# Block sums in the last up tiles, two 8 KB weight slots, and raw token tiles on GpSimd in a decoder layer

## The chip, the cores and the metric

The kernel runs on one core of one Trainium2 chip. Its time is the device time of one execution in microseconds; lower is better. A core has TensorE (matrix products; PE in the profile, PEld for its weight loads), VectorE (DVE), ScalarE (ACT), GpSimd (POOL) and SyncE (SP), whose queue issues all the large DMAs of this kernel. Each engine runs its own instructions in a fixed order and waits at semaphores for the others.

## The reference, cut to what matters

One layer over 1024 tokens of width 1024, all float32. Three parts add to the residual stream `x`; the change touches the first two.

```python
x = x + 0.5 * (silu(h1 @ w_gate) * (h1 @ w_up)) @ w_down        # FFN1, h1 = rms_norm(x), hidden width 2816
h = rms_norm(x); p = h @ w_in                                   # latents, FoX q, k, v, forget logits, two gates
x = x + (sigmoid(g_mla) * (mla(p) @ w_a) + sigmoid(g_fox) * (fox(p) @ w_b)) @ w_o
x = x + 0.5 * (silu(h2 @ w_gate) * (h2 @ w_up)) @ w_down        # FFN2, h2 = rms_norm(x)
```

Float32 accuracy is kept on 16-bit products by writing each operand as a high and a low half and taking three products: high by high, high by low, low by high.

## The kernel before, in words

**Order on the engines.** The kernel is written as Python that emits instructions. A planner then lays them out per engine: among the instructions whose inputs and buffers are ready in its own model of time, the earliest emitted goes first. So an instruction can be placed well before the point where the code emits it. Three means hold it back: `in_order(engines)` chains everything in a block per engine, `follow(name)` puts one instruction behind a named one on its engine, and buffers: `slot(tag)` takes one of the 8 KB tiles "u" (8 of them), "v", "act" and "wd" (4 each), and an instruction that fills one waits until its last reader is done. PSUM has two double banks "a", three banks "b" and one "g".

**FFN1's start** (`start`, inside `in_order` for ScalarE, VectorE and TensorE). For each of eight token tiles `norm_steps` gives steps: `q` (squares), `s` (scale), `t` (eight transposes into a double bank, L612), `h` (ScalarE copies the bank as 16-bit high half, L620 and L622), `l` (VectorE subtracts to get the low half, L637 and L639) and, for tiles 4 to 7, `r` (`raw`, ScalarE copies the bank once more as float32, L629 and L631). `token_sums` then builds sums of token quarters from high, low and raw tiles on VectorE (L879, L883) for a product scheme that needs seven block products instead of eight.

**FFN1's up part.** The hidden width is cut into 22 tiles of 128. Tiles 2 to 21 go through `tile(j)` in `up_tiles` and `hidden_tile`: seven steps of 12 products each (L1045), with the operands of the next tile made by `pair_sums`: three GpSimd sums (L1020 to L1022), seven splits (L166 on ScalarE, L169 on VectorE), and a GpSimd subtract in between (L1034). GpSimd also multiplies gate and up (L1095) and makes the sums of activations of a pair of tiles (`act_sums`, L841), which SP stores (L845). The last step of a tile runs inside the next one. `extra()` at the end of `tile(j)` carries side work: with k = j - 3 it loads one slice of `w_in` and takes the maximum of the one before (L803), and at chosen k calls `in_scales`, which spreads such maxima over all partitions by small TensorE products (`spread_max`, L200, then L208) and turns them into powers of two with short VectorE instructions. At k = 17 (tile 20) it calls the third and the fourth part one after the other; the fourth first reduces two small vectors (L979).

**FFN1's down part** (`ffn_down`). Two halves of K with five blocks each (CK = 5), seven block products each, so 70 steps of 12 products (L1205). Operands are prepared three steps ahead. A block of `w_down` takes one slot, filled by two DMAs (`down_load`, L929), and three or four GpSimd sums make its combinations t1 to t4 (L1177), emitted at the steps that need them: t1 at i = 0, t2 at i = 1, t3 at i = 3, t4 at i = 5. The first five t1 are held behind products of the last up tiles by `follow`. The old rows of `x` are loaded behind the fifth block (L516).

**Input projection** (`in_proj`, `proj_steps`, TensorE in order). Three groups (queries, keys, values) of eight token tiles, each in two halves `h` of 12 products. `in_weights` loads a group's weights as four DMAs of 512 KB into a ring of two buffers (`stgi`, L1320) and splits each (L166, L169). Between the halves run the chains of FoX queries and keys (`fox_qk`, L1407 to L1420) and of the MLA projections (`mla_proj`, L1549 to L1657).

FFN2 runs the same code as FFN1 on other buffers; its second half of the start is `first_half`.

Of the kernel before, what the change touches and what calls it, by code (L numbers as in the profile page):

```python
# [14 lines left out]
AF = mybir.ActivationFunctionType  # L15
ALU = mybir.AluOpType
AX = mybir.AxisListType
# [47 lines left out]
class Layer:  # L65
    def __init__(self, tc, ins, out):
        self.tc = tc
        self.nc = tc.nc
        self.i = ins
        self.out = out  # L70
        self.bcount = 0
        self.opn = 0
        self.products = []


    def psa(self, name="psa"):
# [348 lines left out]
    def first_half(self, norm, p0):  # L425


        pg, pu = self.psbg(), self.psbg()
        n = {t: self.norm_steps(norm, t) for t in range(4, NT)}
        (wg, wu), (hi, lo) = p0["w"], (norm[k][0] for k in ("hi", "lo"))  # L430
        full = lambda t: [n[t][c]() for c in "hlr"]
        both = lambda t: [n[t][c]() for c in "qs"]
        part = lambda o, w, c: self.part(o, w, hi, lo, c)
        both(4)
        part(pg, wg, "H")
        n[4]["t"]()
# [12 lines left out]
        n[7]["t"]()  # L449
        full(7)  # L450
        part(pu, wu, "L")
        self.mark()
        return pg, pu
# [119 lines left out]
    def norm_steps(self, st, t, engine=None):  # L573
# [50 lines left out]
        def raw():  # L624
            if t >= 4 and st["raw"] is not None:
                for k in (0, 4):
                    o, a = st["raw"].rows(k, 4, s), rows(box["ps"], k)
                    if not late:
                        nc.scalar.copy(o, a)  # L629
                    else:  # L630
                        nc.scalar.activation(o, a, AF.Copy, scale=st["s"])  # L631

        def low():
            for k in (0, 4):
# [137 lines left out]
    def up_tiles(self, norm, name, tags, loads, stats, scales, sumd):  # L772
# [4 lines left out]
        def tile(j, ops, tok, finish, mid):  # L777
            if j + 3 < NH:
                loads[j + 3] = self.pair_load(name, j + 3, tags["w"])
            nxt = iter(())  # L780
            if j + 1 < NH:
                nxt = self.pair_sums(loads.pop(j + 1), stats.pop(j + 1), norm, scales, j + 1)
# [12 lines left out]
            box["even"] = e  # L795
            def extra():
                k = j - 3
                if name == "ffn1":
                    load, n, values = self.injobs
                    if 0 < k <= n + 1:  # L800
                        last = self.latest(mybir.EngineType.DVE)
                        col = 1663 + k if k <= n else 1701
                        self.nc.vector.tensor_reduce(  # L803
                            out=self.spare[:, col:col + 1], in_=box.pop("in"), op=ALU.max, axis=AX.X,
                            apply_absolute_value=True,
                        )
# [21 lines left out]
            )  # L828

        return tile  # L830

    def act_sums(self, a, b, dst, last=False):

# [104 lines left out]
    def in_jobs(self):  # L938
# [14 lines left out]
        def values(slot):  # L953
            st = slot[:, :HEADS * HD].rearrange("p (h d) -> p h d", h=HEADS)
            self.nc.sync.dma_start(st, self.i["mla_w_kvb"][0].rearrange("p (h d) -> p h d", h=HEADS)[:, :, HD:])
            self.nc.sync.dma_start(
                self.spare[:, 1703:1704], self.i["mla_kv_lat_norm"][0].rearrange("(p k) -> p k", k=1)
            )
            return slot[:, :HEADS * HD]

        return load, len(cuts), values
# [1 line left out]
    def in_scales(self, part):  # L963

        v = self.nc.vector
        raw, m, ps = self.spare[:, 1664:1680], self.spare[:, 1680:1692], self.psb("mx")
# [8 lines left out]
        small, all3 = self.spare[:, 1692:1700], self.spare[:, 1700:1703]  # L975
        t, wkv, gkv = (all3[:, k:k + 1] for k in range(3))
        last = self.latest(mybir.EngineType.DVE)
        for o, src in ((t, small), (gkv, self.spare[:, 1703:1704])):
            v.tensor_reduce(out=o, in_=src, op=ALU.max, axis=AX.X, apply_absolute_value=True)  # L979
            self.follow(last)  # L980
        self.spread_max(all3, 3, all3, ps)
        v.tensor_tensor(out=wkv, in0=wkv, in1=gkv, op=ALU.mult)
        s, inv = self.pow2(m, 14, self.ws[:, :36])
# [27 lines left out]
    def pair_sums(self, w, stat, norm, scales, j):  # L1011
# [20 lines left out]
        yield split(a11)  # L1032
        yield split(a12)
        pool(out=a12, in0=a12, in1=s2, op=ALU.subtract)  # L1034
        for src in (a21, s2, a12, s3, a22):
            yield split(src)

# [12 lines left out]
    def hidden_tile(self, ops, tok, e, nxt, finish, then, inv, late, mid, extra, col):  # L1050
# [45 lines left out]
        self.products = (self.products + [nc.cur_bb.bb.instructions[-1].name])[-3:]  # L1096
        prep()
        late()
        extra()
# [11 lines left out]
    def ffn_down(self, x, old, name, tags, tail, pending):  # L1111
# [13 lines left out]
        raw, extra, staged, loaded = {}, {}, {}, {}  # L1125

        def weights(k):
            if k >= KT or k in raw:
                return
            w = self.down_load(name, k, self.slot(tags["raw"][k % len(tags["raw"])]))  # L1130
            loaded[k] = self.latest(mybir.EngineType.SP)
            if k % CK % 2 == 0:
                extra[k] = self.slot(tags["extra"]).rearrange("p (k s n) -> p k s n", k=2, s=2)
            e = extra[k - k % CK % 2][:, k % CK % 2]
            raw[k] = dict(
                b11=w[:, 0, 0], b21=w[:, 1, 0], t1=w[:, 0, 1], b22=w[:, 1, 1], t2=e[:, 0], t3=e[:, 1], t4=w[:, 1, 0],
            )

        def acts(c, i, k):

# [20 lines left out]
        def prep(n):  # L1161
# [10 lines left out]
            a = operand(acts(c, i, k), self.down[c][0], after)  # L1172
            b = operand(w[order[i][1]], self.down[c][1], after)
            made = {0: ("t1", "t1", "b11"), 1: ("t2", "b22", "t1"), 3: ("t3", "t2", "b11"), 5: ("t4", "b21", "t2")}
            if i in made:
                o, u, v = (w[s] for s in made[i])
                nc.gpsimd.tensor_tensor(out=o, in0=u, in1=v, op=ALU.subtract)  # L1177
# [9 lines left out]
        for n, (c, i, k) in enumerate(steps):  # L1187
# [6 lines left out]
                self.down.append(self.down_scale(1, mx))  # L1194
            ready.append(prep(n + ahead))
            if n == 1 and name == "ffn1":
                self.load_x(x, old, range(NT), loaded[CK - 1])
# [99 lines left out]
        v.tensor_tensor(out=d2, in0=d2, in1=tmp, op=ALU.add)  # L1297


    def in_weights(self, name, c0, after=()):  # L1300
# [5 lines left out]
        scale = self.win[("lat", "q", "k", "v").index(name)][0]  # L1306
        cols = slice(0, n)
        if name == "lat":
            room = [self.slot("act")[:, :4 * n].rearrange("p (k n) -> p k n", k=4) for _ in range(2)]
            for k, st in zip((0, 4), room):  # L1310
                nc.sync.dma_start(st[:, :, :C_FQ], w_in[:, k:k + 4, :C_FQ])
                nc.sync.dma_start(st[:, :, C_FQ:], w_in[:, k:k + 4, C_FL:C_FL + HEADS])
        for kk in range(KD // 2):
            ks = slice(2 * kk, 2 * kk + 2)
            tag = ("stg", "stg", "whi", "wlo")[kk] if name == "q" else "stg"
            if name == "lat":
# [40 lines left out]

    def proj_steps(self, hT, gates, groups, due, stages, mark):
        nc = self.nc
        for h in range(2 * 3 * NT):  # L1360
            gi, t, half = h // (2 * NT), h // 2 % NT, h % 2
            name, c0 = groups[gi]
            if t == 0 and half == 0:
                w = self.in_weights(name, c0, mark)
# [751 lines left out]
```

## Time and profile before

| what | value |
|---|---|
| three runs | 2092.53, 2095.57, 2091.62 us, median 2092.53 |
| profiled execution | 2089.92 us, its span 2088.1 us |
| instructions | 28654 |
| TensorE busy | 2038.5 us, 98% of the span |
| VectorE, ScalarE, GpSimd busy | 1454.7, 1169.6, 646.0 us |
| DMA | 338.09 MB, mean 162 GB/s |

The span is the stretch of one profiled execution from its first to its last instruction. In the rows that follow, a row of an engine in order of time reads: start, duration, engine, line, operation, output <- input, shape, count, and in brackets how long the engine idled before and whose result ended that. Rows of windows give, for a stretch, the busy time and the count of instructions of each engine, then the granted TensorE clock (1.00 is full), the DMA share and GB/s. Tiles are named by what the program calls them (`s_u` is a slot of tag "u", `op` a split operand, `mx` a bank of `spread_max`).

### The profile page before, as it was taken

What the parts mean: (1) busy time and instruction counts of PE and PEld (TensorE: products, weight loads), DVE (VectorE), ACT (ScalarE), POOL (GpSimd) and SP (SyncE); (2) the same over time, 40 slices, a digit from 0 to 9 for tenths busy, and PEclk for the clock granted to TensorE, in tenths of its full rate; (3) what the DMA queues carried; (4) which work ended last, traced back from release to release, by engine and by line L of the source; (5) the groups of instructions that cost most, each with busy time, mean ns of one, the idle gap of its engine ahead of it and who ended that gap; (6) DMA issues with size and microseconds to landing.
All of it is one profiled execution on the core that took longest, in us unless ns stands there. A gap on an engine that the chain in (4) does not pass through costs nothing.

```text
span 2088.1 us, 28654 instructions
## 1 busy us (share of the span) xinstructions
PE 2038.5 (98%) x10247; PEld 1108.3 (53%) x10247; DVE 1454.7 (70%) x2453; ACT 1169.6 (56%) x1969; POOL 646.0 (31%) x719
## 2 busy tenths in 40 slices
PE   7999999999999999999999999999999999999999
PEld 4444444444446555566666665478544444444445
DVE  7856666778877687557677778864765555458876
ACT  7666665544555444466656775422666666555552
POOL 2454554662200011212222222000154555564300
PEclk9999999999999999999999999999999999999999
DMA  8248675465533466565555675451454564355432
GB/s 227 76 139 268 202 246 177 136 225 180 171 115 142 145 193 186 156 168 167 159 137 133 176 197 160 161 172 61 121 151 142 162 201 123 125 200 209 141 110 113
DMA packets 277496, 338.09 MB, mean 162 GB/s; under 512 B 22105, under 2 KB 206281, under 8 KB 277354
## 3 DMA queue, kind: packets, MB, share of 16 engines
q1 hardware_dynamic: 277354, 336.27, 52.5%
q8 instruction: 80, 1.31, 0.3%
q14 instruction: 62, 0.51, 0.1%
HBM read 242.42 MB, written 93.81 MB: 161 GB/s over the span
## 4 chain that ended last, share of the span: by engine, by line
PE 62%; DVE 10%; ACT 4%; issue 2%; DMA 2%; SPq 0%; POOL 0%; ACTq 0%; DVEq 0%
PE psd L1205 15%; PE pst L1045 10%; PE psb L1045 6%; PE pss L1856 3%; PE pspt L1882 3%; PE psb L158 2%; PE psb L156 2%; PE psb L157 2%; PE psgate L156 2%; PE psgate L158 2%; PE psgate L157 2%; PE pspv L1892 2%; DVE op L169 2%; PE psg L1045 1%; PE psin L156 1%
## 5 line engine op out<-in xcount | busy, mean ns | idle before, releaser
L1045 PEld LDWEIGHTS <-op 128*128 128x128 f16 x3360 | 329.0, 98 | 390.5 <-DVE s_act L1093 1.9
L1205 PE MATMUL psd<-op 128*128 128x512 f16 x1680 | 366.4, 380 | 4.7 <-DVE op L169 3.0
L1205 PEld LDWEIGHTS <-op 128*128 128x128 f16 x1680 | 164.8, 98 | 204.8 <-issue 9.0
L169 DVE SCALAR_TENSOR_TENSOR op<-s_u,s_v,op 128x512 f16<-128x512 f32 x170 | 150.6, 895 | 90.2 <-ACT op L166 89.7
L1045 PE MATMUL pst<-s_u,op 128*128 128x512 f16 x720 | 166.3, 381 | 1.4 <-DVE s_act L1093 1.4
L169 DVE SCALAR_TENSOR_TENSOR op<-s_act,s_wd,op 128x512 f16<-128x512 f32 x130 | 123.6, 963 | 62.2 <-ACT op L166 62.2
L1045 PE MATMUL pst<-s_v,op 128*128 128x512 f16 x720 | 165.2, 379 | 1.3 <-DVE s_u L1093 1.3
L166 ACT ACTIVATE op<-s_u,s_v 128x512 f16<-128x512 f32 x170 | 118.0, 715 | 83.8 <-PE psd L1205 72.1
L1863 ACT ACTIVATE s_act<-pss,nm 128x128 f32<-128x128 f32 (+7 forms) x128 | 94.6, 740 | 83.8 <-DVE nm L1860 78.0
L1902 POOL COPY atp<-cmb 64x128 f32<-64x128 f32 x64 | 19.6, 306 | 325.5 <-DVE cmb L1900 325.5
L1856 PE MATMUL pss<-s_wd 96*128 96x256 f32 (+5 forms) x480 | 115.2, 364 | 0.0
L1020 POOL TENSOR_TENSOR sums<-s_u 128x512 f32<-128x512 f32 x20 | 25.8, 1292 | 252.2 <-PE psa L612 157.4
L169 DVE SCALAR_TENSOR_TENSOR s_v<-pspt,s_v 128x512 f16<-128x512 f32 (+1 forms) x160 | 96.0, 629 | 9.4 <-ACT s_v L166 8.2
L1882 PE MATMUL pspt<-ident,s_act 128*128 128x128 f32 x576 | 91.5, 279 | 7.0 <-ACT s_act L1863 4.5
L156 PE MATMUL psgate<-s_u,whi 128*128 128x512 f16 x256 | 97.7, 382 | 0.4 <-ACT z L1693 0.4
L157 PE MATMUL psgate<-s_u,whi 128*128 128x512 f16 x256 | 97.1, 379 | 0.0
L158 PE MATMUL psgate<-s_u,wlo 128*128 128x512 f16 x256 | 97.1, 379 | 0.0
L166 ACT ACTIVATE op<-s_wd 128x512 f16<-128x512 f32 x70 | 50.4, 721 | 80.0 <-PE psd L1205 77.1
L166 ACT ACTIVATE op<-s_act,s_wd 128x512 f16<-128x512 f32 x130 | 88.8, 710 | 11.3 <-POOL s_act L1034 4.8
L166 ACT ACTIVATE s_v<-pspt 128x512 f16<-128x512 f32 (+1 forms) x160 | 82.6, 552 | 21.9 <-PE pspt L1882 20.1
L1860 DVE TENSOR_REDUCE nm<-pss 128x1 f32<-128x128 f32 (+7 forms) x128 | 93.6, 748 | 1.4
L1045 PE MATMUL psb<-s_u,op 128*128 128x512 f16 x360 | 82.6, 379 | 0.0
(546 smaller groups left out, 4513.3 us busy)
## 6 DMA issues: line engine op xcount, KB each, us to landing
sumd<-s_u SPq DMA_DIRECT2D x20, 1024.0 KB
s_wd<-in_ffn_w_down_dram SPq DMA_DIRECT2D x32, 512.0 KB
s_u<-in_w_in_dram SPq DMA_DIRECT2D x15, 1024.0 KB
sumd<-s_wd SPq DMA_DIRECT2D x13, 1024.0 KB
s_wd<-fd SPq DMA_DIRECT2D x48, 256.0 KB
s_act<-in_ffn_w_down_dram SPq DMA_DIRECT2D x22, 512.0 KB
s_wd<-sumd SPq DMA_DIRECT2D x14, 768.0 KB
s_u<-sumd SPq DMA_DIRECT2D x14, 768.0 KB
```

The source lines that it names most:

```text
L156: mm(out, lhsT=lh, rhs=rh, start=start, stop=False)
L157: mm(out, lhsT=lh, rhs=rl, start=False, stop=False)
L158: mm(out, lhsT=ll, rhs=rh, start=False, stop=stop)
L166: self.nc.scalar.activation(hi, src, AF.Copy, scale=scale)
L169: self.nc.vector.scalar_tensor_tensor(out=lo, in0=src, scalar=scale, in1=hi, op0=ALU.mult, op1=ALU.subtract)
L1045: mm(out, lhsT=a[:, k, :], rhs=b[:, k, :], start=start and k == 0 and i == 0, stop=k == n - 1 and i == 2, skip_group_check=True,)
L1205: nc.tensor.matmul(o, lhsT=u[:, r], rhs=w, start=start and m == 0, stop=k == CK - 1 and m == 2, skip_group_check=True,)
L1856: mm(ps[:, b:e], lhsT=a[:, q], rhs=bb[:, b:e], start=k == 0, stop=k == len(passes) - 1)
L1860: nc.vector.tensor_reduce(out=nm, in_=ps[:, :n], op=ALU.max, axis=AX.X, negate=True)
L1863: nc.scalar.activation(pn[:, :n], ps[:, :n], AF.Exp, bias=nm, accum_out=rs[:, i, j:j + 1])
L1882: nc.tensor.transpose(pt[:, o:o + P], pr[m][:, kt * P:(kt + 1) * P], self.ident)
L1892: mm(po[:, :256], lhsT=v[:, kt, :], rhs=slab[:, s, c, e * 256:(e + 1) * 256], start=kt == 0 and s == 0, stop=False,)
```

## The change

1. `tile(j)` of FFN1 takes down blocks 0, 1, 2 at the start of tiles 18, 19, 20 and blocks 3 and 4 at that of tile 21 (`block`: slot and two DMAs each), and emits t1, t2 and t3 of each at the tile's `extra()` (`block_sums`): those of blocks 0 to 2 behind `self.behind`, the subtract L1034 of the next pair, those of blocks 3 and 4 behind the product L1095 of tile 20. `ffn_down` then makes only t4 of these blocks.
2. `in_scales` becomes five calls: the reductions of L979 are a part of their own at k = 12, and the last part, with its small products, moves from k = 17 to k = 18 (tile 21). The DMA of `mla_kv_lat_norm` moves from k = 16 to k = 4.
3. The keys' and the values' weights are loaded by `in_load` at halves 1 and 17, each as two DMAs of 1 MB into two "u" slots, instead of four through `stgi`.
4. In FFN1's start `raw` is no longer a ScalarE copy out of the bank: GpSimd adds the high and the low half of the tile (two adds of 128x512 a tile). FFN2 keeps the copies, emitted ahead of the low half's subtract instead of behind it.

```diff
-        full = lambda t: [n[t][c]() for c in "hlr"]
+        full = lambda t: [n[t][c]() for c in "hrl"]
...
-                    if not late:
-                        nc.scalar.copy(o, a)
+                    if engine is None:
+                        nc.scalar.copy(o, rows(box["ps"], k))
                     else:
-                        nc.scalar.activation(o, a, AF.Copy, scale=st["s"])
+                        engine.tensor_tensor(out=o, in0=h.rows(k, 4, s), in1=l.rows(k, 4, s), op=ALU.add)
...
         def tile(j, ops, tok, finish, mid):
+            k = j - (NH - 4)
+            early = () if name == "ffn2" or k < 0 else (k,) if k < 3 else (3, 4)
+            for k in early:
+                self.blocks[name, k] = self.block(name, k, "act" if k < 4 else "u", "v")
...
             def extra():
                 k = j - 3
+                for b in early:
+                    self.block_sums(self.blocks[name, b], self.behind if b < 3 else self.product_of[0])
...
-                    for part, at in enumerate((9, 13, 17, 17)):
+                    for part, at in enumerate((9, 13, 17, 12, 18)):
...
+    def block_sums(self, w, last):
+        for o, u, v in (("t1", "t1", "b11"), ("t2", "b22", "t1"), ("t3", "t2", "b11")):
+            self.nc.gpsimd.tensor_tensor(out=w[o], in0=w[u], in1=w[v], op=ALU.subtract)
+            self.follow(last)
...
+            if (name, k) in self.blocks and c == 0 and i < 5:
+                made = {}
             if i in made:
                 o, u, v = (w[s] for s in made[i])
                 nc.gpsimd.tensor_tensor(out=o, in0=u, in1=v, op=ALU.subtract)
-                if name == "ffn1" and n < CK:
-                    self.follow(self.products[(0, 0, 1, 1, 2)[n]])
...
+    def in_load(self, cuts, tag):
+        w_in = self.i["w_in"][0].rearrange("(k p) n -> p k n", p=P)
+        n = sum(e - b for b, e in cuts)
+        room = [self.slot(tag)[:, :4 * n].rearrange("p (k n) -> p k n", k=4) for _ in range(2)]
+        for k, st in zip((0, 4), room):
+            at = 0
+            for b, e in cuts:
+                self.nc.sync.dma_start(st[:, :, at:at + e - b], w_in[:, k:k + 4, b:e])
+                at += e - b
+        return room
...
+            if h in (1, 17):
+                c = groups[gi + 1][1]
+                rooms[gi + 1] = self.in_load(((c, c + HALF),), "u")
```

More of the change, by code (lines that the diff above doesn't have):

```diff
@@ L72, in __init__ @@
         self.opn = 0
-        self.products = []
+        self.blocks, self.product_of = {}, []
     def psa(self, name="psa"):
@@ L626, in raw @@
                 for k in (0, 4):
-                    o, a = st["raw"].rows(k, 4, s), rows(box["ps"], k)
-                    if not late:
-                        nc.scalar.copy(o, a)
+                    o = st["raw"].rows(k, 4, s)
+                    if engine is None:
+                        nc.scalar.copy(o, rows(box["ps"], k))
                     else:
-                        nc.scalar.activation(o, a, AF.Copy, scale=st["s"])
+                        engine.tensor_tensor(out=o, in0=h.rows(k, 4, s), in1=l.rows(k, 4, s), op=ALU.add)
         def low():
@@ L813, in extra @@
                         )
-                    for part, at in enumerate((9, 13, 17, 17)):
+                        self.nc.sync.dma_start(
+                            self.spare[:, 1703:1704], self.i["mla_kv_lat_norm"][0].rearrange("(p k) -> p k", k=1)
+                        )
+                    for part, at in enumerate((9, 13, 17, 12, 18)):
                         if k == at:
@@ L830, in up_tiles, with block @@
         return tile
+    def block(self, name, k, tag, extra):
+        w = self.down_load(name, k, self.slot(tag))
+        self.loaded = self.latest(mybir.EngineType.SP)
+        if k % (KT // 2) % 2 == 0:
+            self.extra = self.slot(extra).rearrange("p (k s n) -> p k s n", k=2, s=2)
+        e = self.extra[:, k % (KT // 2) % 2]
+        return dict(
+            b11=w[:, 0, 0], b21=w[:, 1, 0], t1=w[:, 0, 1], b22=w[:, 1, 1], t2=e[:, 0], t3=e[:, 1], t4=w[:, 1, 0],
+        )
+    def block_sums(self, w, last):
+        for o, u, v in (("t1", "t1", "b11"), ("t2", "b22", "t1"), ("t3", "t2", "b11")):
+            self.nc.gpsimd.tensor_tensor(out=w[o], in0=w[u], in1=w[v], op=ALU.subtract)
+            self.follow(last)
     def act_sums(self, a, b, dst, last=False):
@@ L955, in values @@
             self.nc.sync.dma_start(st, self.i["mla_w_kvb"][0].rearrange("p (h d) -> p h d", h=HEADS)[:, :, HD:])
-            self.nc.sync.dma_start(
-                self.spare[:, 1703:1704], self.i["mla_kv_lat_norm"][0].rearrange("(p k) -> p k", k=1)
-            )
             return slot[:, :HEADS * HD]
@@ L965, in in_scales @@
         v = self.nc.vector
-        raw, m, ps = self.spare[:, 1664:1680], self.spare[:, 1680:1692], self.psb("mx")
+        raw, m = self.spare[:, 1664:1680], self.spare[:, 1680:1692]
+        small, all3 = self.spare[:, 1692:1700], self.spare[:, 1700:1703]
+        t, wkv, gkv = (all3[:, k:k + 1] for k in range(3))
+        if part == 3:
+            last = self.latest(mybir.EngineType.DVE)
+            for o, src in ((t, small), (gkv, self.spare[:, 1703:1704])):
+                v.tensor_reduce(out=o, in_=src, op=ALU.max, axis=AX.X, apply_absolute_value=True)
+                self.follow(last)
+            return
+        ps = self.psb("mx")
         if part < 3:
@@ L974, in in_scales @@
             return
[L975 to L980, printed above, removed]
         self.spread_max(all3, 3, all3, ps)
@@ L1034, in pair_sums @@
         pool(out=a12, in0=a12, in1=s2, op=ALU.subtract)
+        self.behind = self.latest(mybir.EngineType.Pool)
         for src in (a21, s2, a12, s3, a22):
@@ L1095, in hidden_tile @@
         nc.gpsimd.tensor_tensor(out=e[:, 1], in0=e[:, 1], in1=e[:, 2], op=ALU.mult)
-        self.products = (self.products + [nc.cur_bb.bb.instructions[-1].name])[-3:]
+        self.product_of = self.product_of[-1:] + [nc.cur_bb.bb.instructions[-1].name]
         prep()
@@ L1124, in ffn_down @@
         )
-        raw, extra, staged, loaded = {}, {}, {}, {}
+        raw, staged = {k: b for (f, k), b in self.blocks.items() if f == name}, {}
         def weights(k):
@@ L1129, in weights @@
                 return
[L1130 to L1137, printed above, removed]
+            raw[k] = self.block(name, k, tags["raw"][k % len(tags["raw"])], tags["extra"])
         def acts(c, i, k):
@@ L1196, in ffn_down @@
             if n == 1 and name == "ffn1":
-                self.load_x(x, old, range(NT), loaded[CK - 1])
+                self.load_x(x, old, range(NT), self.loaded)
             if n == (2 * CK if name == "ffn1" else CK):
@@ L1297, in rotate, with in_weights @@
         v.tensor_tensor(out=d2, in0=d2, in1=tmp, op=ALU.add)
-    def in_weights(self, name, c0, after=()):
+    def in_load(self, cuts, tag):
[8 more added lines that the diff above has]
+        return room
+    def in_weights(self, name, c0, after=(), room=None):
         nc = self.nc
@@ L1308, in in_weights @@
         if name == "lat":
[L1309 to L1312, printed above, removed]
+            room = self.in_load(((0, C_FQ), (C_FL, C_FL + HEADS)), "act")
         for kk in range(KD // 2):
@@ L1315, in in_weights @@
             tag = ("stg", "stg", "whi", "wlo")[kk] if name == "q" else "stg"
-            if name == "lat":
+            if room is not None:
                 st = room[kk // 2][:, 2 * (kk % 2):2 * (kk % 2) + 2]
@@ L1359, in proj_steps @@
         nc = self.nc
+        rooms = {}
         for h in range(2 * 3 * NT):
@@ L1363, in proj_steps @@
             if t == 0 and half == 0:
-                w = self.in_weights(name, c0, mark)
+                w = self.in_weights(name, c0, mark, rooms.get(gi))
                 if gi == 0:
                     self.mla_weights()
+            if h in (1, 17):
+                c = groups[gi + 1][1]
+                rooms[gi + 1] = self.in_load(((c, c + HALF),), "u")
             if half == 0:
```

## The prediction

> **What bounds the kernel now.** I read the page first (busy time by engine), then stretches of the span in windows, then the instructions in order of time where a stretch had holes.
>
> ```profile
> PE 2038.5 (98%) x10247; PEld 1108.3 (53%) x10247; DVE 1454.7 (70%) x2453; ACT 1169.6 (56%) x1969; POOL 646.0 (31%) x719
> ```
>
> TensorE bounds it: 98% busy. No edit removes a matrix product, so the change can only win holes of TensorE and the slow clock behind them. The windows show which holes lie where it acts (columns: stretch, its length, busy us and count of PE, PEld, DVE, ACT, POOL, then granted clock, DMA share, GB/s):
>
> ```profile
> core 0: us, PE busy (x) PEld busy (x) DVE busy (x) ACT busy (x) POOL busy (x), PEclk, DMA share, GB/s
> 30.00:45.00 15.00, 10.63 (x56) 5.42 (x55) 10.70 (x17) 12.16 (x21) 1.82 (x3) 1.00 0.66 134
> 420.00:435.00 15.00, 11.81 (x55) 6.33 (x53) 11.74 (x28) 4.60 (x7) 10.50 (x9) 0.89 0.78 274
> 446.00:480.00 34.00, 30.07 (x132) 13.29 (x131) 32.32 (x34) 13.26 (x21) 25.82 (x16) 0.95 0.69 245
> 700.00:850.00 150.00, 142.01 (x729) 81.50 (x728) 112.22 (x315) 68.58 (x168) 26.68 (x78) 0.99 0.60 174
> 1465.00:1480.00 15.00, 14.56 (x79) 7.79 (x77) 11.23 (x22) 13.59 (x27) 1.27 (x1) 1.00 0.98 246
> 1860.00:1930.00 70.00, 69.23 (x323) 31.45 (x321) 58.00 (x69) 34.89 (x53) 39.75 (x27) 1.00 0.67 237
> ```
>
> They are: FFN1's start, its last up tiles, its first down products, the input projection, FFN2's start, and FFN2's change from up to down, which runs the same code on other buffers and idles 0.77 us of 70.
>
> **Part 1: block sums inside the last up tiles, scales in two halves (420 to 435).** The loads hardly move: the old kernel already issues them there.
>
> ```profile
> 390.12 17.44 SPq L929 DMA_DIRECT2D s_act<-in_ffn_w_down_dram  x2
> ```
>
> What moves is GpSimd's order. Around tile 20 the sums t1 to t3 of two blocks (L1177; the last two of the six stand in the first row) and sums of `act_sums` (L841) ran ahead of the subtract of the last pair (L1034):
>
> ```profile
> 416.98 2.94 POOL L1177 TENSOR_TENSOR s_v<-s_v,s_act 128x512 f32<-128x512 f32 x2
> 419.88 1.26 POOL L841 TENSOR_TENSOR s_u<-s_u 128x512 f32<-128x512 f32 x1
> 421.10 1.26 POOL L1034 TENSOR_TENSOR s_act<-s_act,sums 128x512 f32<-128x512 f32 x1
> ```
>
> ```profile
> 427.80 1.65 PE L200 MATMUL mx<-ident,s_wd 128*128 128x128 f32 x6 [3.19 <-DVE s_wd L979]
> 429.24 2.15 PE L1045 MATMUL pst<-s_u,op 128*128 128x512 f16 x5
> 431.23 2.75 PE L1045 MATMUL pst<-s_v,op 128*128 128x512 f16 x12
> 433.82 2.75 PE L1045 MATMUL psb<-s_u,op 128*128 128x512 f16 x12
> ```
>
> The late subtract held ScalarE's and VectorE's splits, VectorE came late to L979, and six small products of `in_scales` stood in TensorE's queue in front of five large ones: 3.19 us idle. The five then took 431.23 - 429.24 = 1.99 us, 0.40 each; the next twelve take 433.82 - 431.23 = 2.59, 0.216 each: half speed. The window's clock of 0.89 makes that 0.11 x 15 = 1.65 us. Together 4.8. Removed here: both reductions of L979 go to k = 12, five tiles earlier (two small instructions, in tiles where TensorE waits for nothing); the small products go to tile 21, where their inputs are long ready; the sums of blocks 0 to 2 follow the pair's subtract. I count **-4.8**; the low end is 0, the hole returning elsewhere. The moved `mla_kv_lat_norm` DMA is one issue 12 tiles earlier on SP, hidden by the tiles between. GpSimd does the same fifteen sums; nine now run in tiles 18 to 20, where six ran in tile 20 alone, 3 x 1.27 = 3.8 us a tile (1.27 as L841 and L1034 above), into this hole of an ordinary tile:
>
> ```profile
> 384.59 1.28 POOL L1020 TENSOR_TENSOR sums<-s_act 128x512 f32<-128x512 f32 x1 [5.18 <-DVE op L169]
> ```
>
> 5.18 covers 3.8, if the block has landed; if not, L1020 to L1022 and the product L1095 wait behind it (a rival below). On SP the loads wait for an `act` slot as they did (17.44 us in the row above), with the stores of `act_sums` behind them.
>
> **Part 2: the first down products (446 to 480).** TensorE idles 34 - 30.07 = 3.9, and clock 0.95 costs 0.05 x 34 = 1.7: 5.6 us.
>
> ```profile
> 463.53 1.24 PE L1205 MATMUL psd<-op 128*128 128x512 f16 x5 [0.39 <-DVE op L169]
> 466.20 7.00 PE L1205 MATMUL psd<-op 128*128 128x512 f16 x31 [1.43 <-DVE s_wd L208]
> 475.31 0.48 PE L1205 MATMUL psd<-op 128*128 128x512 f16 x1 [2.11 <-DVE op L169]
> ```
>
> VectorE is the releaser, busy 32.32 of 34, because its splits run long beside GpSimd's sums: 1.75 against 0.74 undisturbed, while an instruction fed from PSUM (L1103) keeps 0.74 in the midst of a GpSimd sum:
>
> ```profile
> 453.33 1.75 DVE L169 SCALAR_TENSOR_TENSOR op<-s_wd,op 128x512 f16<-128x512 f32 x1
> 455.00 0.74 DVE L1103 SCALAR_TENSOR_TENSOR s_u<-pst,s_wd,s_u 128x512 f32<-128x512 f32 x1
> ```
>
> ```profile
> 452.83 3.38 POOL L841 TENSOR_TENSOR s_u<-s_u 128x512 f32<-128x512 f32 x2
> ```
>
> ```profile
> L169 DVE SCALAR_TENSOR_TENSOR op<-s_u,s_wd,op 128x512 f16<-128x512 f32 x12 | 8.9, 743 | 0.0
> ```
>
> So a collision costs 1.75 - 0.74 = 1.0. Block 4's three sums leave this stretch: -3.0 of VectorE. But the second half of `in_scales` enters it (tile 21 instead of 20): fourteen VectorE instructions that wait for the small products, L982, L985 and twelve taken at 0.15 each, like L180:
>
> ```profile
> L982 DVE TENSOR_TENSOR s_wd<-s_wd 128x1 f32<-128x1 f32 x1 | 0.8, 839 | 0.0
> L985 DVE TENSOR_SCALAR ws<-ws 128x12 f32<-128x12 f32 x1 | 0.7, 701 | 0.0
> ...
> L180 DVE TENSOR_SCALAR ws<-s_wd 128x1 f32<-128x1 f32 x2 | 0.3, 147 | 0.0
> ```
>
> 0.84 + 0.70 + 12 x 0.15 = 3.3 us. Ends: the loss grows by 3.3, or it goes as in FFN2, whose row keeps TensorE busy with GpSimd at work 39.75 of 70 (gain 5.6). The stretch is like FFN2's in its sums and unlike it in the scales, so I take the middle, **-1.2**. L841, the t4 sums and block 5's stay in this stretch and keep colliding.
>
> **Part 3: keys' and values' weights in two slots (700 to 850).** Eight loads of 512 KB through two ring buffers become four of 1 MB; the last two of each four, which waited for a ring buffer, go out some fifteen halves earlier. SP carries fewer issues; the bytes are the same. The eight splits remain: 8 ScalarE copies and 8 VectorE subtracts, at other times.
>
> ```profile
> PE psmt L1634 <- DVE s_v L1623: 5.6, 6, 2.6
> PE psft L1417 <- DVE qk L1412: 2.4, 2, 1.2
> ```
>
> ```profile
> 733.68 1.28 DVE L169 SCALAR_TENSOR_TENSOR s_act<-stgi,ws,s_wd 128x1024 f16<-128x1024 f32 x1
> ```
>
> ```profile
> 743.47 1.15 ACT L166 ACTIVATE s_wd<-stgi,ws 128x1024 f16<-128x1024 f32 x1 [2.59 <-DMA stgi<-in_w_in_dram]
> ```
>
> The last two rows are splits of the keys' weights. Two such subtracts in a row push the query chain (L1412) back, and the last split, 2.59 us late by its DMA, goes ahead of the MLA chain to L1623; the values repeat it. All of it is 8.0 us (150 - 142.01). With the data early, each of the two late splits leaves the chain: 2 x 1.28 = 2.6; of the 2.4 behind doubled splits I take half, as they must still run on a VectorE 75% busy. **-3.8.** Ends: +2.4 (two more doubled bursts) and -8.0. The rooms take four `u` slots until the splits, so the forget gate's tile and the branch weights' loads come later; neither is read before attention.
>
> **Part 4: raw token tiles by GpSimd (30 to 45).** Eight ScalarE copies go, in pairs of 1.27 or 1.07 us, and eight GpSimd adds come.
>
> ```profile
> 31.42 1.27 ACT L631 ACTIVATE s_v<-psa,tk 128x512 f32<-128x512 f32 x2 [1.48 <-DVE s_u L639]
> 32.58 1.07 ACT L620 CAST s_u<-psa 128x512 f16<-128x512 f32 x2
> 35.01 1.07 ACT L629 COPY s_v<-psa 128x512 f32<-128x512 f32 x2 [1.35 <-DVE s_u L637]
> ```
>
> ```profile
> 32.74 1.09 PE L612 MATMUL psa<-ident,y 128*128 128x128 f32 x8 [2.19 <-ACT s_v L631]
> 33.67 1.89 PE L421 MATMUL psb<-s_u,wlo 128*128 128x512 f16 x8
> 36.13 1.09 PE L612 MATMUL psa<-ident,y 128*128 128x128 f32 x8 [0.57 <-ACT s_v L629]
> 37.06 1.89 PE L421 MATMUL psg<-s_u,wlo 128*128 128x512 f16 x8
> 40.56 0.81 PE L421 MATMUL psb<-s_u,whi 128*128 128x512 f16 x3 [1.61 <-ACT s_u L620]
> ```
>
> The raw copy stands between the low half's subtract and the bank's release, so the holes can shrink by 1.27, 0.57 and one pair's 1.07: 2.9 of 4.4. The adds, 8 x 1.27 = 10.2, fit into GpSimd's idle (1.82 busy of 15), but the last four run beside VectorE's token totals, which read two SBUF tiles: up to 4 x 1.0 = 4.0. I take half of 2.9, **-1.5**; ends +4.0 and -4.4. In FFN2 the copies stay on ScalarE and only go ahead of the subtract: the window there idles 0.44, so 0, with ends -0.4 and +1.1 (one pair of copies in the subtract's way).
>
> **A rule against the change.** The Trainium skill, SBUF - State Buffer, section "Who interferes with whom", says that VectorE with two SBUF inputs and a GpSimd instruction that reads SBUF exclude each other for the whole instruction. The trace agrees that L169 suffers and L1103 does not, but shows 1.0 a collision, not the sum's whole 1.27. By the page's rule eight adds would cost up to 10.2 at the start.
>
> **The sum.** 4.8 + 1.2 + 3.8 + 1.5 = 11.3. The profiled execution took 2089.92 (span 2088.1), 2.6 under the median of the runs; the holes are the same in both, so 2092.5 - 11.3 = **2081.2**.
>
> **Rivals.** (a) All holes close: 4.8 + 5.6 + 8.0 + 2.9 = 21.3, 2071.2. For it: FFN2's row. Against: the scales' 3.3 and the remaining splits. Chance 0.13. (b) The start turns to a loss: all eight adds collide, 8 x 1.0 less VectorE's 4.3 idle of 30 to 45 = 3.8 lost instead of 1.5 won: 2086.8. Against: only four can meet the totals. 0.12. (c) The hole returns in tile 21: the small products' maximum meets the saturated VectorE, holds a PSUM bank of the first down products, nothing of 4.8 is won and 3.3 is added: 2092.5 - 5.3 + 3.3 = 2090.5 (5.3 is what parts 3 and 4 win). 0.14. (d) Slower: a block sum placed early waits for its load, with the next pair's sums and the product behind it on GpSimd. It decides once a block lands more than 5.18 - 3.8 = 1.4 us after the subtract; then tiles 18 to 20 each repeat the 4.8 hole and the old one stays: 2092.5 - 5.3 + 3 x 4.8 = 2101.6. For it: loads wait 17 us for a slot. Against: they land in the tile before. 0.14. My forecast: 0.47.
>
> **Numbers.** What this measurement can tell from no change is about 0.2%, 4.2 us. Forecast, (a) and (b) lie beyond: faster 0.72; (c) same 0.14; (d) slower 0.14. The range 2073 to 2095 leaves out about half of (a) and most of (d). The forecast's own range is 2076 to 2087.
>
> **What would show it.** Right: no TensorE idle before the six small products, L1034 of the last pair ahead of that tile's block sums, at most 3 us idle in the first 34 us of down products, ScalarE waiting for no `w_in` load in the input projection, no ScalarE raw copy at the start and token transposes that no longer wait for it. Wrong: GpSimd waiting for a down block, VectorE over 95% busy for longer after the last up tile, new waits of L1417 or L1634 before the keys' group.

## The result, and the profile after

The changed kernel took 2077.57 us (median of 4 runs, 2075.87 to 2080.56) against 2092.89 beside it: ratio 0.9927, 95% interval 0.9909 to 0.9944. The forecast was 2081.2. The profiled execution took 2077.2, its span is 2075.4 against 2088.1. The medians differ by 15.3 us, the two profiled executions by 12.7: that of the kernel before was 3.0 faster than its median, that of the changed kernel 0.4. The profiles explain the 12.7; the other 2.6 lie between executions, and no trace shows them.

The busy times, and the windows shown of before, now of the changed kernel; 680 to 700 is new:

```profile
PE 2034.6 (98%) x10247; PEld 1105.9 (53%) x10247; DVE 1451.3 (70%) x2453; ACT 1165.7 (56%) x1961; POOL 662.1 (32%) x727
```

```profile
core 0: us, PE busy (x) PEld busy (x) DVE busy (x) ACT busy (x) POOL busy (x), PEclk, DMA share, GB/s
30.00:45.00 15.00, 13.95 (x75) 7.47 (x75) 12.27 (x18) 7.70 (x12) 13.32 (x10) 1.00 0.67 132
420.00:435.00 15.00, 15.00 (x74) 7.05 (x73) 7.74 (x11) 7.46 (x12) 8.53 (x6) 1.00 0.74 265
446.00:480.00 34.00, 32.76 (x152) 14.71 (x151) 34.00 (x46) 18.18 (x28) 20.32 (x11) 1.00 0.71 247
680.00:700.00 20.00, 17.36 (x85) 8.45 (x83) 8.43 (x28) 6.63 (x17) 0.10 (x1) 0.91 0.68 222
700.00:850.00 150.00, 145.16 (x757) 84.50 (x756) 118.66 (x328) 72.71 (x183) 32.04 (x95) 1.00 0.53 152
```

and the same place of the program as 680 to 700, in the kernel before, where the input projection starts 9.4 us later:

```profile
689.50:709.50 20.00, 18.23 (x100) 9.61 (x99) 9.72 (x31) 7.29 (x19) 0.27 (x2) 1.00 0.54 173
```

The first four holes shrank: 4.4 us idle to 1.05 at the start, 3.19 to none in the last up tiles, 3.9 to 1.24 in the first down products (with their clock back at 1.00), 8.0 to 4.8 in the input projection. In the down products the window holds a later part of the program than before, as the first product came at 446.77 and now comes at 439.26; between 420 and 446 and between 480 and 500 no product waits, so that 1.24 is the whole. One hole grew: between 680 and 700 TensorE idles 2.6 us instead of 1.8, and its clock falls to 0.91.

Since all runs here execute the same products in the same order between a few marks, the time between two marks tells more than the sum. The table takes the start times of TensorE's instructions from each kernel's timeline: A, the first tile product (`pst`); B, from there to the first down product (`psd`); C, to the first product of the input projection (`psin`); D, to the first of its last three; E, to the first tile product of FFN2; F, to the span's end.

| kernel | A | B | C | D | E | F | span | median of runs |
|---|---|---|---|---|---|---|---|---|
| before | 72.3 | 374.5 | 252.2 | 180.5 | 631.2 | 577.4 | 2088.1 | 2092.89 |
| changed | 69.8 | 369.4 | 250.4 | 175.5 | 632.6 | 577.6 | 2075.4 | 2077.57 |
| changed, second | 70.9 | 369.4 | 251.1 | 175.4 | 631.4 | 576.8 | 2075.1 | 2076.93 |
| changed, third | 71.0 | 369.4 | 252.7 | 175.4 | 634.4 | 577.0 | 2079.9 | 2078.00 |
| block sums undone | 70.9 | 370.4 | 250.6 | 175.8 | 631.5 | 576.6 | 2075.8 | 2079.98 |
| scales undone | 71.0 | 369.6 | 250.8 | 175.8 | 633.0 | 577.3 | 2077.4 | 2077.81 |
| both undone | 70.7 | 372.9 | 255.8 | 175.9 | 635.0 | 577.4 | 2087.6 | 2088.22 |
| rooms undone | 70.5 | 369.4 | 247.3 | 182.2 | 630.2 | 576.3 | 2076.0 | 2082.07 |
| raw undone | 72.9 | 369.5 | 251.6 | 175.4 | 632.2 | 576.8 | 2078.3 | 2079.17 |
| loads held | 70.0 | 369.4 | 246.5 | 176.1 | 632.1 | 577.7 | 2071.8 | 2073.65 |
| loads held, second | 70.4 | 369.5 | 246.8 | 176.3 | 630.6 | 577.4 | 2070.9 | 2073.62 |
| held, splits spread | 70.9 | 369.4 | 247.0 | 176.5 | 630.8 | 577.0 | 2071.6 | 2076.54 |
| held, scale first | 70.9 | 370.1 | 247.3 | 177.5 | 631.1 | 577.7 | 2074.6 | 2076.88 |

From before to changed: A -2.5, B -5.0, C -1.8, D -5.0, E +1.4, F +0.2, together -12.7. A scatters by about 1 us; the clock of the first 20 us differs too, from 0.74 to 1.00, but whether that makes it is open. E holds attention, which the change does not touch, and scatters from 630.2 to 635.0. Two things show in it: at the end of a chain that starts at a load (`sg<-gd`) TensorE waits 2.1 us in the third trace of the changed kernel, 1.1 in the first, 0.6 and nothing in the two with the loads held; and the third trace has a clock of 0.91 from 1360 to 1380, the one with both undone 0.83 from 1310 to 1330. So a single span says little below 3 us; the stretches B and D repeat within 0.2 us for the same kernel. Medians compare within one set of runs only: the undone sums, scales and rooms are one set, the second row of changed stands with both undone, loads held and splits spread, the third with the last three kinds.

### The profile page after: what moved, and what is told of

The parts are those of the page before. It is cut to its first block, busy times and chain, and to the rows that moved or that the text cites. A ratio compares the mean times of both kernels' runs of the same rounds, so it can differ in the third digit from the quotient of the medians.

```text
span 2075.4 us, 28646 instructions
## 1 busy us (share of the span) xinstructions
PE 2034.6 (98%) x10247; PEld 1105.9 (53%) x10247; DVE 1451.3 (70%) x2453; ACT 1165.7 (56%) x1961; POOL 662.1 (32%) x727
## 4 chain that ended last, share of the span: by engine, by line
PE 78%; DVE 12%; ACT 4%; DMA 3%; issue 2%; SPq 0%; POOL 0%; ACTq 0%; DVEq 0%; POOLq 0%
PE pst L1071 19%; PE psd L1224 15%; PE psb L1071 11%; PE psg L1071 3%; PE pss L1888 3%; PE pspt L1914 3%; DVE op L169 2%; PE psgate L156 2%; PE psgate L158 2%; PE psgate L157 2%; PE pspv L1924 2%; PE psb L158 2%; PE psb L156 2%; PE psb L157 2%; PE psin L158 1%
## 5 line engine op out<-in xcount | busy, mean ns | idle before, releaser
L169 DVE SCALAR_TENSOR_TENSOR op<-s_u,s_v,op 128x512 f16<-128x512 f32 x170 | 149.9, 891 | 90.0 <-ACT op L166 89.5
L169 DVE SCALAR_TENSOR_TENSOR op<-s_act,s_wd,op 128x512 f16<-128x512 f32 x130 | 119.9, 934 | 57.0 <-ACT op L166 57.0
L169 DVE SCALAR_TENSOR_TENSOR s_v<-pspt,s_v 128x512 f16<-128x512 f32 (+1 forms) x160 | 95.9, 629 | 9.4 <-ACT s_v L166 8.2
L1071 PE MATMUL psb<-s_wd,op 128*128 128x512 f16 x360 | 82.6, 379 | 0.0
```

Source lines behind the costliest of these rows:

```text
L169: self.nc.vector.scalar_tensor_tensor(out=lo, in0=src, scalar=scale, in1=hi, op0=ALU.mult, op1=ALU.subtract)
L1071: mm(out, lhsT=a[:, k, :], rhs=b[:, k, :], start=start and k == 0 and i == 0, stop=k == n - 1 and i == 2, skip_group_check=True,)
```

## The experiments

### Which half of part 1 removed the stall

Three kernels: the block sums back in the down stage, `in_scales` back in tile 20, and both.

```diff
-            early = () if name == "ffn2" or k < 0 else (k,) if k < 3 else (3, 4)
+            early = ()
...
                 nc.gpsimd.tensor_tensor(out=o, in0=u, in1=v, op=ALU.subtract)
+                if name == "ffn1" and n < CK: self.follow(self.products[(0, 0, 1, 1, 2)[n]])
```

> The changed kernel with the loads and sums of the five down blocks back inside the down stage, behind the products of the last tiles; the halves of in_scales stay at 12 and 18. Theory A (the place of the six small products made the stall of 420 to 435, GpSimd's order made the losses of 446 to 480): no wait of the small products, the down products idle and slow as before (4.4 us of the 12.7), so about 2082 us. Theory B (GpSimd's order made both): the stall comes back too, 4.4 + 5.0 us, about 2087 us.

```diff
-                    for part, at in enumerate((9, 13, 17, 12, 18)):
+                    for part, at in enumerate((9, 13, 17, 17, 17)):
```

> The changed kernel with both halves of in_scales in tile 20 again (at 17); the early block sums stay. Theory A: the six small products wait again in tile 20 for the late maximum, 3 to 5 us, less what the down products win by having the scales' fourteen small VectorE instructions out of the way (up to 3.3): 2077 to 2082 us. Theory B: VectorE is no longer late there, since the pair's subtract is ahead on GpSimd: the wait is under 0.5 us, and the down products win up to 1.2 us: 2076.5 to 2078 us.

> The changed kernel with the block sums back in the down stage and the scales back in tile 20, both at once. Theory (either one alone keeps the stall of 420 to 435 away, since the small products must be in tile 20 and GpSimd late for it): 5.0 us come back there and up to 4.4 in the first down products, in all 7 to 9.4 us over the changed kernel. Rival (the effects of the two single runs add up): 0.9 there and 1.3 in the down products, about 2 us over the changed kernel.

TensorE's waits from 420 to 500 (total, times, longest), first with both undone, then with the sums alone undone, then the scales alone:

```profile
PE mx L200 <- DVE s_wd L994: 3.2, 1, 3.2
PE psd L1224 <- DVE op L169: 2.5, 2, 2.1
PE psd L1224 <- DVE s_wd L208: 1.4, 1, 1.4
```

```profile
PE psd L1224 <- DVE op L169: 2.4, 2, 1.8
PE pst L1071 <- DVE s_u L1119: 0.8, 1, 0.8
```

```profile
PE psd L1224 <- DVE s_wd L208: 0.8, 1, 0.8
PE psd L1224 <- DVE op L169: 0.3, 1, 0.3
```

With both undone the waits of before are back to a tenth of a microsecond (there 3.19, 2.50 in two and 1.43). With either half alone the six small products wait for nothing. Undoing the scales alone costs nothing that shows: B +0.1, and 1.1 us of waits among the first down products, where the changed kernel idles 1.24. Its theory B holds. Undoing the sums alone costs 0.9 us in B and 2.4 us of waits among the down products; no stall, as its theory A had it, but only 1.2 of the 4.4 us that it expected back there. The last pair's subtract is late there all the same, behind the block sums: it starts at 419.72, and at 421.10 in the kernel before. So the stall needed two conditions at once, a subtract of the last pair behind block sums and small products in that tile, and each half of part 1 removes one. The rival that the two single effects add up (2 us) is out: both undone stand 11.3 us above the changed kernel in their set, 2088.22 against 2076.93. That is more than the 7 to 9.4 expected. In the traces 3.4 lie in B and 4.7 in C, and up to the end of the projection they differ by 8.3 (875.2 against 866.9 us), within it; behind that E was long in this trace (635.0), with 0.17 x 20 = 3.4 us of slow clock. The stall's window with both undone has the idle time of before and a full clock:

```profile
420.00:435.00 15.00, 11.84 (x62) 6.22 (x61) 13.41 (x30) 5.24 (x8) 10.23 (x8) 1.00 0.88 320
```

### The rooms: what they win and what they cost

```diff
-            if h in (1, 17):
+            if False:
```

> The changed kernel with keys' and values' weights loaded through the two ring buffers again. Theory: the 5.1 us won in 700 to 850 go, and so does the new loss at 680 to 690 (2.6 us of lead, 1 MB loads of the rooms ahead of the last loads of mla_w_kvb in SP's queue): 2077.6 + 5.1 - 2.6 = about 2080.1 us, the hole at 690 as before (1.6 us). Rival: the loss at 680 to 690 comes from the order of ScalarE alone and stays: 2077.6 + 5.1 = about 2082.7 us.

Both effects stand in the table: without the rooms D is 182.2 instead of 175.4 to 175.5, and C is 247.3 instead of 250.4 to 252.7. The rooms win 6.8 us inside the projection and lose 3 to 5 in front of it (4.1 in the mean of three traces), in idle time and slow clock. About half of the 6.8 is slow clock: without the rooms TensorE idles 8.15 us of 700 to 850 instead of 4.84, and the clock is 0.98, which costs 3.0 us more.

By times, 2082.07 stands 4.3 above the undone scales of the same set, whose trace is within 0.5 us of the changed kernel's second up to the end of the projection. That lies between the theory (2.5) and the rival (5.1), and the six runs spread over 8 us (2077.81 to 2085.72), so the median cannot choose; the trace does. In it the loss goes with the rooms, so ScalarE's order alone does not make it. How they make it, in the changed kernel; SP's loads first, then ScalarE's and TensorE's waits:

```profile
658.50 0.43 SPq L1327 DMA_DIRECT2D s_u<-in_w_in_dram  x1
663.45 0.39 SPq L1327 DMA_DIRECT2D s_u<-in_w_in_dram  x1
...
676.20 0.38 SPq L1571 DMA_DIRECT2D stgm<-in_mla_w_kvb_dram  x1
677.57 0.57 SPq L1327 DMA_DIRECT2D s_u<-in_w_in_dram  x1
683.24 0.33 SPq L1571 DMA_DIRECT2D stgm<-in_mla_w_kvb_dram  x1
686.18 0.43 SPq L1327 DMA_DIRECT2D s_u<-in_w_in_dram  x1
```

```profile
682.61 0.62 ACT L1572 CAST s_v<-stgm 128x512 fp32r<-128x512 f32 x1 [4.30 <-DMA stgm<-in_mla_w_kvb_dram]
683.13 1.07 ACT L620 CAST s_u<-psa 128x512 f16<-128x512 f32 x2
```

```profile
PE psb L156 <- ACT s_u L620: 1.9, 1, 1.9
```

The program has the values' loads at half 17 of the projection, but nothing except free slots held them back, and the planner put all four 1 MB loads ahead of the projection's first product (689.7 us), in among the loads of `mla_w_kvb`. ScalarE waits 4.30 us for one of these, and 2.73 without the rooms; behind that copy stand the last tile's high halves (L620), and TensorE waits for them. The next kernel keeps each of these loads behind the last instruction that the program gave SP before it:

```diff
-        room = [self.slot(tag)[:, :4 * n].rearrange("p (k n) -> p k n", k=4) for _ in range(2)]
+        last = self.latest(mybir.EngineType.SP); room = [self.slot(tag)[:, :4 * n].rearrange("p (k n) -> p k n", k=4) for _ in range(2)]
...
                 self.nc.sync.dma_start(st[:, :, at:at + e - b], w_in[:, k:k + 4, b:e])
+                if tag == "u": self.follow(last)
```

> The changed kernel with each of the four 1 MB loads of keys' and values' weights kept behind the last instruction that the program gave SP before it, so that the keys' two follow the last load of mla_w_kvb and the values' two go out during the projection. Theory (these loads ahead of mla_w_kvb in SP's queue make the hole before the projection): the hole falls from 2.6 to about 1.0 us idle, the clock there stays 1.00, ScalarE's wait for the third stgm load falls from 4.3 to about 2.7 us, the projection keeps its gain: 2.5 to 3.5 us under the changed kernel. Rival (ScalarE's order makes the hole whatever the loads do): the same time as the changed kernel within 0.5 us. Third way: the values' loads come too late for their splits and 2 to 4 us are lost in 780 to 830, so nothing is won in sum.

> The changed kernel once more, beside the next three on the same chip, so that they can be set against it: 0.7% under the kernel before (ratio 0.993), with 2.6 us idle and a clock near 0.91 in the 20 us around the last loads of mla_w_kvb.

The same loads and copy in this kernel, and its window:

```profile
674.99 0.56 SPq L1571 DMA_DIRECT2D stgm<-in_mla_w_kvb_dram  x1
680.54 0.33 SPq L1571 DMA_DIRECT2D stgm<-in_mla_w_kvb_dram  x1
680.93 0.43 SPq L1326 DMA_DIRECT2D s_u<-in_w_in_dram  x1
...
748.32 1.42 SPq L1326 DMA_DIRECT2D s_u<-in_w_in_dram  x2
```

```profile
680.13 0.62 ACT L1572 CAST s_v<-stgm 128x512 fp32r<-128x512 f32 x1 [1.91 <-DMA stgm<-in_mla_w_kvb_dram]
```

```profile
680.00:700.00 20.00, 19.66 (x106) 10.24 (x104) 9.58 (x32) 8.32 (x21) 1.20 (x6) 1.00 0.67 215
```

TensorE's wait is gone (0.34 idle), the clock is 1.00, C falls from 251.1 to 246.5, and D rises by only 0.7. The time is 2073.65 against 2076.93 beside it; repeated:

> The kernel with the keys' and values' loads held behind those of mla_w_kvb, for the next one to be set against: 2.5 to 3.5 us under the changed kernel.

> The changed kernel, beside the next three on the same chip, so that they can be set against it: about 0.7% under the kernel before.

2073.62 against 2078.00. So 3.3 and 4.4 us under the changed kernel, where 2.5 to 3.5 were expected; against the kernel before the ratios are 0.9920 (0.9906 to 0.9933) and 0.9917 (0.9904 to 0.9930). It is the fastest version that was run.

### Spreading the weight splits

```diff
-            if h in (8, 24):
-                mark = [self.latest(e) for e in (mybir.EngineType.Activation, mybir.EngineType.DVE)]
+            if h in (8, 10, 12, 14, 24, 26, 28, 30):
+                marks = (marks + [[self.latest(e) for e in (mybir.EngineType.Activation, mybir.EngineType.DVE)]])[-4:]
```

Each of a group's four splits then follows its own mark.

> As the kernel with the loads held back, and the four weight splits of a group no longer placed at one point (behind halves 8 and 24) but two halves apart each (8, 10, 12, 14 and 24, 26, 28, 30). Theory (four ScalarE copies and VectorE subtracts in a row push the query chain back, two waits of 1.6 us of the transposes psft for it): these waits go, up to 3.3 us under the kernel with the loads held back alone. Rival (the splits only change places, and the ones left behind push the MLA chain, as before the change): within 1 us of it.

TensorE's waits of over 1 us each from 700 to 850, with the loads held, then with the splits spread as well:

```profile
PE psft L1449 <- DVE qk L1444: 3.3, 2, 1.6
```

```profile
PE psb L1604 <- DVE s_v L1593: 3.0, 1, 3.0
PE psft L1449 <- DVE rs_y L110: 1.4, 1, 1.4
```

In the trace the rival holds: the two waits of 1.6 went, and one of 3.0 us came in the MLA chain (L1593 feeds L1604) and one of 1.4 in the query chain. D is 176.5 instead of 176.1, the span 2071.6 instead of 2071.8. The median is 2.9 higher (2076.54 against 2073.65), more than the rival's 1 us; the profiled run was the fastest of its five, and what made the others slower is open.

### The start

```diff
-                    if engine is None:
+                    if not late:
                         nc.scalar.copy(o, rows(box["ps"], k))
                     else:
-                        engine.tensor_tensor(out=o, in0=h.rows(k, 4, s), in1=l.rows(k, 4, s), op=ALU.add)
+                        nc.scalar.activation(o, rows(box["ps"], k), AF.Copy, scale=st["s"])
```

> The changed kernel with the raw token tiles copied from PSUM by ScalarE again, as before the change. Theory (the start wins 4.0 us up to the last part of the second half and loses 1.5 of it at the weights of tile 1, whose scale stands behind VectorE's token totals): the last psb part starts about 3 to 4 us later than in the changed kernel, the first tile product 1.5 to 2.8 us later, the time is 1.5 to 2.8 us longer. Rival (the lead is slack that a later wait for a load swallows): the same time within 0.5 us.

The last `psb` part starts at 41.11 instead of 36.56 to 37.71, A is 72.9 instead of 69.8 to 71.0, and B, the 370 us behind it, is the same to 0.1: nothing swallows the lead there. This trace has a clock of 0.89 from 30 to 45, the changed kernel 1.00, so up to 1.65 us of the difference can be slow clock; the kernel before, at 1.00, has 72.3. An earlier kernel with these copies left out the scale of the first of the four tiles, so that it computes something else; its trace has 72.6 (clock 0.89 too) and the same B, its runs a median of 2079.52 beside 2077.81 for the scales undone. The times, 2079.17 against 2078.00, cannot separate 1.2 us from none (ratios to before 0.9945, 0.9933 to 0.9957, and 0.9940, 0.9928 to 0.9952). Why only half of the 4 us arrives, in the changed kernel on TensorE and VectorE (a short row left out):

```profile
47.99 0.39 PE L156 MATMUL psa<-s_u,whi 128*128 128x512 f16 x1 [0.46 <-ACT whi L241]
49.31 0.39 PE L158 MATMUL psa<-s_u,wlo 128*128 128x512 f16 x1 [0.71 <-DVE wlo L246]
```

```profile
40.43 2.05 DVE L908 TENSOR_TENSOR s_v<-s_v,s_u 128x1024 f32<-128x1024 f32 x1
42.92 0.60 DVE L510 TENSOR_SCALAR bg<-bg 128x16 f32<-128x16 f32 x1 [0.44 <-DMA bg<-in_b_gate_dram]
43.51 1.21 DVE L908 TENSOR_TENSOR s_v<-s_v,s_u 128x1024 f32<-128x1024 f32 x1
...
45.78 0.41 DVE L208 TENSOR_REDUCE bst<-mx 128x1 f32<-128x256 f32 x1
```

and VectorE before:

```profile
44.84 0.17 DVE L510 TENSOR_SCALAR bg<-bg 128x16 f32<-128x16 f32 x1
...
46.38 0.42 DVE L208 TENSOR_REDUCE bst<-mx 128x1 f32<-128x256 f32 x1
```

L208 leads to the scale of tile 1's weights. TensorE came 4.0 us earlier, L208 only 0.6, since VectorE's token totals stand ahead of it. A last kernel puts the scale and the splits ahead of them:

```diff
+            if not ready:
+                p1["spread"]()
+                p1["hi"]()
+                p1["lo"]()
             total(1, 0)
             high(3, 0)
             low(3, 0)
-            if not ready:
-                p1["spread"]()
-                p1["hi"]()
-                p1["lo"]()
```

> As the kernel with the loads held back, and the scale and splits of tile 1's weights ahead of the token totals 1 on VectorE and ScalarE (the same instructions in another order). Theory (in the changed kernel the maximum L208 stands behind two totals L908 and a split L898 on VectorE, so TensorE waits 0.46 and 0.71 us for whi and wlo): both waits go, the first tile product comes 31.7 to 32.2 us after the last psb part starts, instead of 33.3, and the time is about 1.2 us shorter. Rival (the totals, now later, keep the next weight splits or the products of the next tiles waiting): the waits move into 55 to 75 us and the time is the same within 0.5 us.

TensorE's idle times from 38 to 95 us are now these:

```profile
60.20 0.49 PE L200 MATMUL mx<-ident,s_wd 128*128 128x128 f32 x2 [1.65 <-ACT s_wd L939]
...
91.37 2.76 PE L1071 MATMUL pst<-s_v,op 128*128 128x512 f16 x12 [1.97 <-DVE s_u L1119]
```

The first tile product comes 33.7 us after the last `psb` part, not 32: the two waits are gone, a wait of 1.65 stands at 60 us, and the one at 91 us grew from 1.3. The rival has the right mechanism and too small a price: B is 0.7 longer, D 1.2, the median 3.3 above the kernel with the loads held (2076.88 against 2073.62), where it said the same time. Why D grew stays open.

## Why the prediction was right, and where its terms were off

The forecast of faster held, and the measured time lies in its own range (2076 to 2087). The terms, against the marks:

- **Part 1, -4.8.** B fell by 5.0, by the mechanism named. The text took both halves as needed; each alone is enough to remove the stall. The sign it listed shows on GpSimd, the last pair's subtract ahead of that tile's block sums:

```profile
411.76 1.72 POOL L1059 TENSOR_TENSOR s_act<-s_act,sums 128x512 f32<-128x512 f32 x1 [1.89 <-DVE op L169]
413.43 1.27 POOL L854 TENSOR_TENSOR s_act<-s_act 128x512 f32<-128x512 f32 x1
...
425.01 1.41 POOL L854 TENSOR_TENSOR s_act<-s_act 128x512 f32<-128x512 f32 x1 [1.38 <-DMA s_act<-in_ffn_w_down_dram]
```

  The last row is the sign of rival (d), a sum that waits for its load. It came in tile 21 behind the last pair, and no one waited for it; the fifth block's sum waits 0.78 us for its load at 450.94. The 1.65 of slow clock does not come with the stall each time: with both halves undone the same 3.2 us stall stood in a window with a clock of 1.00, and B rose by 3.4 only.
- **Part 2, -1.2: the term that was mis-sized.** Idle and clock loss went from 5.6 to 1.24, so -4.4, near the good end. How long VectorE needs here is the time from the start of its last L1119 before the down products (L1093 in the kernel before) to that of the first L1232 (L1213), which takes down products out of their bank: 23.42 us before, 23.40 with both halves undone, 20.32 with the scales alone undone, 21.54 in the changed kernel (438.80 to 460.34). Three of the scales' rows in it:

```profile
445.24 0.14 DVE L184 TENSOR_SCALAR ws<-ws 128x1 int32<-128x1 int32 x1
445.30 0.14 DVE L185 TENSOR_SCALAR ws<-ws 128x1 int32<-128x1 int32 x1
445.36 0.14 DVE L182 TENSOR_SCALAR ws<-ws 128x1 int32<-128x1 int32 x1
```

  So the early block sums win 3.1 there, as forecast for block 4's (3.0). The scales do stand in this stretch, as forecast, but make it 1.2 longer and not 3.3: that is the term that was wrong. It added durations of 0.15, but the rows start 0.06 us apart; and without the scales VectorE waits 1.1 us in this stretch (0.6 at L1027, 0.5 at L169), which they fill. On TensorE they cost nothing that shows (1.24 us idle with them, 1.1 without), and the 1.7 of slow clock went. VectorE is busy 34.00 of 34, the "wrong" sign of over 95%, and TensorE still has nearly all its operands in time. The mechanism was right, and the size was not.
- **Part 3, -3.8.** The projection alone gave -5.0 in D (and 6.8 against rooms undone), ScalarE waits there for no `w_in` load, and the doubled bursts cost 3.3 instead of 2.4. Of the 5.0, 3.2 are idle time (8.0 to 4.8) and the rest is slow clock, 0.99 in the window before, which the text did not count here. What it missed as well is the other side: it counted what SP carries less of, and not what stands behind the four 1 MB loads in its queue. They cost about 4 us in front of the projection, so that the net was about -2.7 by the traces of rooms undone (6.8 less 4.1).
- **Part 4, -1.5.** A fell by 2.5 in the two profiles compared, by 1.9 to 3.0 against raw undone, part of which can be slow clock. Half taken was right, and for the reason given in kind, VectorE; in place, it was the totals ahead of L208. Three collisions are seen on VectorE: L908 at 2.05 against 1.21, L605 at 1.75 (30.85 us) against 1.27, and L510 at 0.60 against 0.17, 1.75 us in all. GpSimd pays as well, its last three adds taking 1.78 each where the first five took 1.32:

```profile
38.15 5.34 POOL L631 TENSOR_TENSOR s_v<-s_u 128x512 f32<-128x512 f16 x3
```

  The 10.2 us that the prediction worked out from the Trainium skill (SBUF - State Buffer, section "Who interferes with whom"), and the 4.0 taken as the end, were far too much.
- **FFN2's order, 0.** TensorE idles 0.40 us in the 20 us around FFN2's start (1450 to 1470) and idled 0.44 before (1465 to 1480).

The mis-sized terms partly cancel: in the two profiles compared, 3.2 more from part 2, 1.2 more inside part 3, 1.0 more at the start and 0.2 from part 1, against 2.6 lost in front of the projection and 1.6 in E and F; 1.4 in sum, the 12.7 won less the 11.3 forecast. That these cancel is luck. The forecast also took the profiled execution's gain for that of the medians, which is 15.3. Rivals (b), (c) and (d) did not happen, nor did (a): 1.05, 1.24 and 4.8 us idle remain in the holes that it closes. In (b) the sum gives 2081.2 + 1.5 + 3.8 = 2086.5, not 2086.8, which changes nothing.

## What to carry to other kernels

When a load is given a buffer of its own, its slot no longer holds it back: look at which small loads now stand behind it in the queue, and tie it to the point where the program means it. Before pricing many short instructions on a saturated engine, take the distance between their starts and not their durations (0.06 against 0.14 us here), and compare two kernels at the same place of the program and not at the same time. A stall that needs two conditions goes away with either, so undo the parts singly and together before crediting one.

## What the runs showed of the hardware

A VectorE instruction of 128x16 elements that takes 0.17 us (L510 above) took 0.60 beside GpSimd's adds of 128x512, and in the second trace of the changed kernel 1.06:

```profile
43.57 1.06 DVE L510 TENSOR_SCALAR bg<-bg 128x16 f32<-128x16 f32 x1
```

In both it ends with the last of the adds: at 43.52 where the three adds shown above end at 43.49, and at 44.63 where they end at 44.59. The Trainium skill, SBUF - State Buffer, section "Who interferes with whom", says that an instruction of this kind can take the port pair that the two engines share, and that the one that comes second is blocked for the whole of the other's instruction. The trace fits that for this short one: it pays by the rest of an add (1.78 us each here), not by its own length.

The same stall of TensorE did not always cost the clock. Idle time of 3.2 us stood in a window with 0.89 before, and with both halves undone in one with 1.00. At the end of attention 1.6 us of 20 showed 0.83 in that run (1310 to 1330) and 1.00 in the changed kernel (1300 to 1320). In front of the projection 2.8 us of 20 showed 0.83 in the third trace of the changed kernel, and 3.2 showed 1.00 with the sums undone. The windows of the last two, in this order:

```profile
680.00:700.00 20.00, 17.16 (x82) 8.70 (x81) 6.53 (x17) 5.85 (x15) 0.00 (x0) 0.83 0.69 222
680.00:700.00 20.00, 16.76 (x95) 8.90 (x93) 8.84 (x25) 8.24 (x20) 0.00 (x0) 1.00 0.70 224
```

What the clock costs comes in steps: 0.11 x 15 = 1.65, 0.05 x 34 = 1.7, 0.09 x 20 = 1.8, and 0.17 x 20 = 3.4, twice as much. The Trainium skill, TensorE: Matmul & The Clock Gate, section "Part 1: The HAM clock gate (the 'warmup' mystery)", has a free-running window of about 3.4 us, and half clock after at least one idle window. Half clock for 3.4 us is the step of 1.7 seen here, and with a free-running window it depends on the phase whether a gap is seen. That idle time of 1.6 and 2.8 us, less than a window, brought the slow clock does not fit that sentence; the measurement decides. A term for slow clock behind 1.6 to 3.2 us of idle time is then one to give with both ends, 0 and 3.4 here.
